# Opening of a two-layer trunk: raw indexer products for four K-tiles, x loaded between modulation tiles, another plan of early chunks

## The chip, the cores and the metric

The kernel runs on one core of a Trainium2 chip. A core has TensorE (PE: matmuls; PEld is its weight load), VectorE (DVE), ScalarE (ACT), GpSimd (POOL), SyncE (SP, which here issues most transfers) and 16 DMA engines. Matmuls accumulate in PSUM, which here is used as eight banks of 128 x 512 fp32: four under the tag "pj", four under the tag "px". The metric is the device time of one execution in microseconds. Each engine works off its instructions in the order in which the program issues them; between engines, semaphores order the work.

## The reference

Two layers (DEPTH 2) of a decoder trunk, 512 tokens, width 2048, fp32:

```python
c_act = silu(c)
for l in range(DEPTH):
    mod = c_act @ w_mod[l] + b_mod[l]               # 2048 x 6144
    shift, scale, gate = split(mod, 3)
    h = rmsnorm(x, norm_gain[l]) * (1 + scale) + shift
    proj = h @ w_in[l]                              # 2048 x 7504
    q_a, k_a, v_a, g_a, q_i, k_i, w_i, q_b, k_b, v_b, g_b = split(proj)
    # group A: indexer (q_i, k_i, w_i) picks 128 keys a query, softmax attention, gate g_a
    # group B: retention of q_b, k_b (rotary), v_b, group norm, gate g_b
    x = x + gate * (concat(y_a, y_b) @ w_out[l])
```

with `rmsnorm(x, g) = x * rsqrt(mean(x*x) + eps) * g`. The factor rsqrt(...) is one number per token and is called rstd here. Shift and scale (with gain) are one number per row of the transposed x.

## The kernel before

**Tiling.** Everything is kept transposed: x as 16 K-tiles of 128 model rows x 512 tokens. fp32 products are made of three fp32r matmuls: a weight w and an activation h are each split into a high part (a copy rounded to fp32r) and a low part (the rest), and wh·hh + wh·hl + wl·hh is summed in PSUM. The high half is made by ScalarE (`split_hi`, line 324; for h, `make_h0`, line 625), the low half by VectorE (`split_lo`, line 334; line 631). Weights come in chunks of up to 1024 columns a partition (`load_chunk`), three tiles of each kind in a ring.

**Modulation.** Shift and scale of layer 0 need 32 tiles of 1 MB from w_mod, one for the shift and one for the scale of each K-tile. VectorE multiplies each with silu(c), broadcast over the partitions (`cb`), and sums along the row (`mod_add`, line 417). Tiles in halves are two such steps. `mod0_loads` issues their transfers, at most four tiles ahead of the sums and into tiles that are free: two of their own, and the arena tiles in which later K-tiles of h will stand. When both sums of a K-tile are there, its h can be made: x is multiplied by rstd (`make_xr`, line 619), ScalarE makes the high part and h itself (lines 625, 629), VectorE the low part (631).

**Opening (`start`).** SP first loads all 16 tiles of x and the positions, then modulation tiles and the first chunks in turn. ScalarE squares x; sums of squares go through TensorE (`row_sums`, line 603), filler matmuls keep it active (`warm`, line 568); `rstd_col` makes 1/sqrt and broadcasts it (line 585). Two units of the bias table (`indicators` on ScalarE, line 894; `unit_mm`, 904; `unit_end`, 911) are made in the gaps. Then K-tile 0 is normalised (`make_h`) and the early plan begins.

**The early plan.** As not all K-tiles are there, projections are done in pieces, listed by hand in PLAN. ("S", c) is chunk c of the group with key, value, indexer key and indexer weights: two K-tiles, 24 matmuls of 336 columns, four PSUM banks "pj" held from S0 to S7. ("E", i, a, b) is K-tiles a to b of 256 columns: for i < 4 of the indexer's queries q_i (384 tokens, as the first 128 need no selection), for i from 4 to 7 of the retention's q and k (512 tokens); each K-tile takes six matmuls, on two banks "px". The result of a first piece is copied to SBUF (`keep`, line 1525), later pieces are added (`more`, line 1540), and the rest of K-tiles, from EARLY[i] on, comes after the plan in full groups (`joined`, line 1532).

**The pacing.** The loop over WORK issues for each plan item: the splits of its weights, its matmuls, the next chunk's transfers and splits, then modulation steps (`mod_step`), then the evacuation. Every item has a cost (1.85 per K-tile of S, 1.36 per K-tile of E); for each RMOD = 4.0 of cost one modulation step is issued, each RBIAS = 6.0 one bias unit. An item whose K-tiles are not yet there forces steps ("forced").

## Time and profile before

| | |
|---|---|
| median of 3 runs | 1851.62 us (1850.3 to 1852.84) |
| the profiled execution's own time | 1849.68 us |
| span of its trace | 1847.9 us, mean granted clock 0.994 |
| TensorE busy in the span | 1821.7 us (99%) |
| VectorE, ScalarE busy | 1384.4 us (75%), 888.0 us (48%) |
| bytes moved | 304.55 MB, mean 165 GB/s |
| modulation sums on VectorE (line 417, 2048 columns) | 2.28 to 2.35 us each |

The profile is of one execution. Its rows give a line of the program, engine, operation, output and input names with shape, a count, busy time and the mean of one; then the idle time ahead of it and what released it. A busy TensorE is not one at its peak: matmuls are pipelined, so their durations overlap, and how many there are counts as much as how long they are.

### The profile page before, as it was taken

How to read it: one execution, taken by the hardware profiler on the slowest of the kernel's cores; microseconds unless marked ns; L12 is line 12 of the kernel's file. 1: busy time of each engine (PE TensorE's matmuls, PEld its weight loads, DVE VectorE, ACT ScalarE, POOL GpSimd, SP SyncE). 2: the span in 40 equal slices, each digit the busy share in tenths (PEclk: the TensorE clock that was granted, in tenths of full speed). 3: DMA queues.
4: the chain of work that ended last, by engine and by line, in shares of the span. 5: the costliest groups of instructions: out<-in, count | busy, mean ns of one | idle time of the engine just before them, and what ended most of it. 6: DMA issues, size and time to landing. Idle time of an engine off the chain costs nothing.

```text
span 1847.9 us, 26300 instructions
## 1 busy us (share of the span) xinstructions
PE 1821.7 (99%) x9644; PEld 1562.9 (85%) x9644; DVE 1384.4 (75%) x2438; ACT 888.0 (48%) x1708; POOL 70.8 (4%) x184
## 2 busy tenths in 40 slices
PE   7999999999999999999999999999999999999998
PEld 7878888888888888888899988888888888889998
DVE  7996699787867846777776699377875686369886
ACT  7668943564546532422235542344444554245443
POOL 0001000000000000100000000000000000000111
PEclk7999999999999999999999999999999999999999
DMA  9995533333454547789864323444534354333554
GB/s 371 364 321 178 165 88 92 109 114 95 123 186 123 174 147 236 233 281 308 304 208 129 103 80 100 142 124 147 155 120 124 93 185 135 102 92 109 149 151 130
DMA packets 175762, 304.55 MB, mean 165 GB/s; under 512 B 16960, under 2 KB 92864, under 8 KB 172048
## 3 DMA queue, kind: packets, MB, share of 16 engines
q1 hardware_dynamic: 171328, 295.23, 50.5%
q0 software_dynamic: 4160, 7.41, 1.6%
q8 instruction: 76, 1.25, 0.3%
q14 instruction: 54, 0.44, 0.1%
q10 hardware_dynamic: 144, 0.22, 0.0%
HBM read 289.18 MB, written 13.63 MB: 164 GB/s over the span
## 4 chain that ended last, share of the span: by engine, by line
PE 83%; DVE 2%; ACT 2%; DMA 1%; issue 1%; SPq 0%; DVEq 0%; ACTq 0%
PE pj L390 15%; PE pj L391 15%; PE pj L392 15%; PE pj L398 6%; PE pj L397 6%; PE pj L396 6%; PE p L1356 3%; PE p L1355 3%; PE p L1354 3%; PE ptr L177 1%; PE pdot L1028 1%; DVE wl L334 1%; PE pdot L1030 1%; ACT wh L324 1%; PE plg L1250 1%
## 5 line engine op out<-in xcount | busy, mean ns | idle before, releaser
L324 ACT ACTIVATE wh<-wf 128x1024 fp32r<-128x1024 f32 (+2 forms) x277 | 284.7, 1029 | 586.9 <-PE pj L391 390.1
L334 DVE TENSOR_TENSOR wl<-wf,wh 128x1024 fp32r<-128x1024 f32 (+2 forms) x277 | 326.6, 1180 | 289.1 <-ACT wh L324 282.5
L390 PE MATMUL pj<-h,wh 128*128 128x512 f32 (+1 forms) x1280 | 488.4, 382 | 1.9 <-ACT bt L911 1.7
L391 PE MATMUL pj<-h,wh 128*128 128x512 f32 (+1 forms) x1280 | 485.9, 380 | 2.6 <-DVE h L631 2.6
L392 PE MATMUL pj<-h,wl 128*128 128x512 f32 (+1 forms) x1280 | 485.7, 379 | 0.5 <-DVE wl L334 0.5
L390 PEld LDWEIGHTS pj<-h,wh 128*128 128x128 f32 x1280 | 240.6, 188 | 44.9 <-issue 2.5
L391 PEld LDWEIGHTS pj<-h,wh 128*128 128x128 f32 x1280 | 240.6, 188 | 42.1 <-DVE h L631 3.8
L392 PEld LDWEIGHTS pj<-h,wl 128*128 128x128 f32 x1280 | 240.5, 188 | 41.4 <-DVE wl L334 1.1
L396 PE MATMUL pj<-wh,h 128*128 128x512 f32 (+1 forms) x616 | 234.6, 381 | 4.1 <-ACT h L625 3.4
L397 PE MATMUL pj<-wl,h 128*128 128x512 f32 (+1 forms) x616 | 233.6, 380 | 0.7 <-DVE wl L334 0.7
L398 PE MATMUL pj<-wh,h 128*128 128x512 f32 (+1 forms) x616 | 232.6, 380 | 0.2 <-DVE h L631 0.2
L396 PEld LDWEIGHTS pj<-wh,h 128*128 128x128 f32 x616 | 116.5, 189 | 26.7 <-ACT h L625 3.9
L397 PEld LDWEIGHTS pj<-wl,h 128*128 128x128 f32 x616 | 116.5, 189 | 20.3 <-DVE wl L334 1.1
L398 PEld LDWEIGHTS pj<-wh,h 128*128 128x128 f32 x616 | 116.2, 189 | 20.4 <-DVE h L631 0.4
L417 DVE CUSTOM_DVE_ANT_0 mw<-mw,cb 128x1024 f32<-128x1024 f32 (+1 forms) x64 | 93.0, 1453 | 7.0 <-POOL mp L416 5.6
L417 DVE CUSTOM_DVE_ANT_0 mw<-mw,cb,mp 128x1024 f32<-128x1024 f32 x68 | 88.3, 1298 | 12.4 <-POOL md L416 7.9
L392 PE MATMUL pj<-y,wl 128*128 128x512 f32 x240 | 93.4, 389 | 0.0
L391 PE MATMUL pj<-y,wh 128*128 128x512 f32 x240 | 93.4, 389 | 0.0
L390 PE MATMUL pj<-y,wh 128*128 128x512 f32 x240 | 93.4, 389 | 0.0
L1262 ACT ACTIVATE bias<-bias,mx 128x128 f32<-128x128 f32 (+1 forms) x64 | 35.9, 561 | 65.3 <-DVE mx L1261 64.6
L1036 DVE SCALAR_TENSOR_TENSOR iacc<-relu,wi,iacc 128x384 f32<-128x384 f32 (+2 forms) x96 | 55.5, 613 | 10.1 <-ACT relu L1034 7.2
L894 ACT ACTIVATE ind<-pos,pt 128x512 bf16<-128x512 f32 (+3 forms) x128 | 61.4, 553 | 0.1
(549 smaller groups left out, 3077.3 us busy)
## 6 DMA issues: line engine op xcount, KB each, us to landing
wf<-in_w_in_dram SPq DMA_DIRECT2D x155, 512.0 KB, 3.7
mw<-in_wmod_dram SPq DMA_DIRECT2D x136, 512.0 KB, 5.7
wf<-in_w_in_dram SPq DMA_DIRECT2D x136, 256.0 KB, 3.1
mw<-in_wmod_dram SPq DMA_DIRECT2D x28, 1024.0 KB, 8.6
wf<-in_w_out_dram SPq DMA_DIRECT2D x32, 512.0 KB, 5.3
...
```

The source lines that it names most:

```text
L324: act(h[:, :n], wf[i][:, :n], AF.Copy)
L334: tt(lo[:, :n], wf.pop(i)[:, :n], f(whl[i][:, :n]), op=OP.subtract)
L390: mm(q, wh[:, o:o + P], ah, start=s0, stop=False)
L391: mm(q, wh[:, o:o + P], al, start=False, stop=False)
L392: mm(q, wl[:, o:o + P], ah, start=False, stop=s1)
L396: mm(q, ah[:, n * P:(n + 1) * P], wh[:, o:o + g.N], start=s0, stop=False)
L397: mm(q, ah[:, n * P:(n + 1) * P], wl[:, o:o + g.N], start=False, stop=False)
L398: mm(q, al[:, n * P:(n + 1) * P], wh[:, o:o + g.N], start=False, stop=s1)
L417: nc.vector.tensor_tensor_reduce(w[:, lo:hi], w[:, lo:hi], cb[:, lo:hi], scale=ng(l, k, 1) if q == 1 else 1.0, scalar=init, op0=OP.mult, o ...
L894: act(v, tab["pos"][:, :w], AF.Sign, bias=tab["pt"][:, col:col + 1], scale=-1.0)
L1036: stt(a[:, :w], r[:, :w], L["WI"][:, c0:c0 + 1], a[:, :w], op0=OP.mult, op1=OP.add)
L1354: mm(dst[m], wh[:, c], bh, start=k == 0 and (own or m == 0), stop=False)
```

## The change

In the opening, the 768 columns of the indexer's queries that belong to E0, E1 and E2 are multiplied for K-tiles 0 to 3 with x·scale before rstd is known, in a group "R" of four chunks of 128 x 768 (NRAW = 3, RAW = 4). `raw_h` makes x·scale, split in high and low, 384 tokens wide, with two more columns that hold the shift; `raw_mm` does 18 matmuls of 386 columns per K-tile on six banks (four "pj", two "px"); `raw_end` copies the six sums to SBUF. Since the sum over K of w·(x·scale·rstd + shift) is rstd times the raw sum plus the shift's column, `raw_join` multiplies by rstd and adds that column and the next piece's sum, when K-tiles 4 to 7 of E0 to E2 are joined.

x is loaded in four lots (1, 3, 6, 6 tiles), each between modulation tiles (`loads`); the squares follow in pairs, in four lots. rstd is known after the last lot; K-tiles 0 to 3 are normalised after that, in a row, by `make_h`. A third bias unit is made in the opening. The first plan item runs when four K-tiles are there. RMOD is 4.5. E0 and E1 go to K-tile 8 early, where they went to 6. Tiles of three early chunks are no longer taken from the general pool (FREE), and the values of h for K-tiles 0 and 1 no longer from VectorE (HVA).

```diff
 DEBUG = False
-PLAN = [("S", 0, 0), ("E", 0, 0, 2, 0), ("S", 0, 1), ("E", 0, 0, 2, 1), ("E", 1, 0, 2),
-        ("E", 2, 0, 2), ("E", 3, 0, 2), ("E", 4, 0, 3), ("E", 5, 0, 3), ("S", 1), ("E", 6, 0, 4), ("E", 7, 0, 4),
-        ("E", 0, 2, 6), ("E", 1, 2, 6), ("S", 2), ("E", 2, 2, 8), ("E", 3, 2, 8), ("S", 3),
-        ("S", 4), ("E", 6, 4, 12), ("E", 7, 4, 12), ("S", 5), ("E", 4, 3, 12), ("E", 5, 3, 12), ("S", 6), ("S", 7)]
+RAW = 4
+NRAW = 3
+
+
+PLAN = [("S", 0), ("S", 1), ("E", 4, 0, 4), ("E", 5, 0, 4), ("E", 6, 0, 4), ("E", 7, 0, 4), ("E", 3, 0, 4), ("S", 2),
+        ("E", 0, 4, 8), ("E", 1, 4, 8), ("E", 2, 4, 8), ("E", 3, 4, 8), ("S", 3), ("E", 6, 4, 8), ("E", 7, 4, 8),
+        ("S", 4), ("S", 5), ("E", 4, 4, 12), ("E", 5, 4, 12), ("E", 6, 8, 12), ("E", 7, 8, 12), ("S", 6), ("S", 7)]
 NE = 8
 EARLY = [max(it[3] for it in PLAN if it[0] == "E" and it[1] == i) for i in range(NE)]
-FREE = (2, 3, 4)
-RMOD = 4.0
+RMOD = 4.5
 RBIAS, KBIAS = 6.0, 3
 REST = [(0, 2, k) for k in range(16)] + [(1, q, k) for k in range(16) for q in (0, 1)] + [(1, 2, k) for k in range(16)]
-HVA = 2
 M0AHEAD = 4
 MX0 = 2
-WA, WS, WL = 24, 4, 8
+WA, WS = 24, 24
 C_ID, C_C, C_CAUS, C_INV, C_THR, C_BLK, C_ONE, C_END = 0, 128, 144, 272, 273, 274, 278, 406
...
     mpart = {}
-    steps0 = [(b, lo, lo + D // 2) for b in range(4) for lo in (0, D // 2)] + [(b, 0, D) for b in range(4, 2 * KT)]
-    m0 = {"load": 0, "add": 0, "mw": 0}
+    whole0 = [b for b in range(4, 2 * KT) if b != 2 * RAW - 1]
+    steps0 = [(b, lo, hi) for b in range(2 * KT) for lo, hi in (((0, D),) if b in whole0 else ((0, D // 2), (D // 2, D)))]
+    m0 = {"load": 0, "add": 0, "mw": 0, "lim": 0}
     m0_tile, m0_last = {}, {}
     def mod0_loads(lim=None):
+        if lim is None:
+            lim = m0["lim"]
         while m0["load"] < len(steps0):
             n = m0["load"]
             b, lo, hi = steps0[n]
             done = steps0[m0["add"]][0] if m0["add"] < len(steps0) else 2 * KT
-            if lim is not None and n >= lim or b >= done + M0AHEAD:
+            if n >= lim or b >= done + M0AHEAD:
                 break
             if lo == 0:
                 keys = [("mw", m0["mw"] % MWBUFS)] + [("HP", j) for j in range(b // 4 + 1, KT // 2)]
         return X[k]
     def make_h0(k, xr):
-        hv = G("hv") if k < HVA else xr
         hh, hl = HLT(k, "h")
         act(hh, xr, AF.Identity, bias=mod_col(0, 0, k), scale=mod_col(0, 1, k))
-        if k < HVA:
-            ts(hv, xr, mod_col(0, 1, k), mod_col(0, 0, k), op0=OP.mult, op1=OP.add)
-        else:
-            act(hv, xr, AF.Identity, bias=mod_col(0, 0, k), scale=mod_col(0, 1, k))
+        act(xr, xr, AF.Identity, bias=mod_col(0, 0, k), scale=mod_col(0, 1, k))
         yield
-        tt(hl, hv, f(hh), op=OP.subtract)
+        tt(hl, xr, f(hh), op=OP.subtract)
         Hh[k], Hl[k] = hh, hl
         yield
+    raw = {}
+
+    def raw_h(k):
+
+        hh, hl = G("rh0", F32R)[:, :TI + 2], G("rl0", F32R)[:, :TI + 2]
+        x, a, b = X[k][:, TOPK:], mod_col(0, 1, k), mod_col(0, 0, k)
+        act(hh[:, :TI], x, AF.Copy, scale=a)
+        act(hh[:, TI:], b.to_broadcast([P, 2]), AF.Copy)
+        stt(hl[:, :TI], x, a, f(hh[:, :TI]), op0=OP.mult, op1=OP.subtract)
+        tt(hl[:, TI:], b.to_broadcast([P, 2]), f(hh[:, TI:]), op=OP.subtract)
+        return hh, hl
+
+    def raw_mm(k, hh, hl):
+        if not k:
+            raw["ps"] = [psum.tile([P, T], F32, name="praw", tag="pj" if n < 4 else "px") for n in range(2 * NRAW)]
+        wh, wl = whl.pop(k)
+        for n, ps in enumerate(raw["ps"]):
+            q, c = ps[:, :TI + 2], slice(n * P, (n + 1) * P)
+            mm(q, wh[:, c], hh, start=k == 0, stop=False)
+            mm(q, wh[:, c], hl, start=False, stop=False)
+            mm(q, wl[:, c], hh, start=False, stop=k == RAW - 1)
+
+    def raw_end():
+        for n, ps in enumerate(raw.pop("ps")):
+            t = raw[n // 2, n % 2] = G("part")
+            act(t[:, :TI + 2], ps[:, :TI + 2], AF.Copy)
+
+    def raw_join(part, key, ps):
+
+        if key in raw:
+            r = raw.pop(key)
+            t = part[key] = r[:, :TI]
+            tt(t, t, state["rstd"][:, TOPK:], op=OP.mult)
+            stt(t, ps, r[:, TI:TI + 1], t, op0=OP.add, op1=OP.add)
+        else:
+            tt(part[key], ps, part[key], op=OP.add)
+
     def start():
         rot, bias = rot_tables(), bias_tables()
-        for k in range(KT):
-            load_x(k)
-        dma(posi, bass.AP(tensor=positions.tensor, offset=positions.offset, ap=[[0, P], [1, T]]))
-        mod0_loads(4)
-        ahead(2, 0)
-        mod0_loads(8)
-        ahead(5, 0)
+        done = 0
+
+        def loads(k):
+            for n in ((0, 1), (4, 5), (8,), (10,))[k]:
+                mod0_loads(n + 1)
+            ahead(k + 1, 0)
+            for j in (range(1), range(1, 4), range(4, 10), range(10, KT))[k]:
+                load_x(j)
+            if k == 0:
+                dma(posi, bass.AP(tensor=positions.tensor, offset=positions.offset, ap=[[0, P], [1, T]]))
+            for n in ((2, 3), (6, 7), (9,), (11, 12))[k]:
+                mod0_loads(n + 1)
+
+        loads(0)
+        loads(1)
         warm(WA)
         act(cs, cst[:, C_C:C_C + KT], AF.Silu)
         act(sm("dummy", 1), cs[:, :1], AF.Sqrt, bias=eps, scale=0.0)
         bias_parts()
         pc = [bcast_c(i) for i in range(4)]
-
-        def put_c(i):
+        for i in range(4):
             v = cb[:, i * T:(i + 1) * T]
             if i % 2:
                 nc.vector.tensor_copy(v, pc[i])
             else:
                 act(v, pc[i], AF.Copy)
-        put_c(1)
-        put_c(3)
+        act(onesr, ones, AF.Copy)
         ind, pend = {}, []
-        def get_ind(u):
-            ind[u] = indicators(*UNITS[u])
-
-        def begin(u):
-            pend.append(unit_mm(*UNITS[u], ind[u]))
-
-        def flush(n=0):
-            while len(pend) > n:
+        def flush():
+            while pend:
                 unit_end(*pend.pop(0))
-
-        pss = psum.tile([P, T], F32, name="prs", tag="pj")
-        ssq, col = G("ssq"), 0
-        for k in range(KT):
-            q = G("sq") if k else ssq
-            act(q, X[k], AF.Square)
-            if k in (3, 5):
-                put_c(k - 3)
-            if k % 3 == 0 and 0 < k < KT - 1:
-                col = row_sums(pss, q, col)
-                warm(WS if k < 12 else WL)
-            elif k:
-                tt(ssq, ssq, q, op=OP.add)
-        col = row_sums(pss, ssq, col)
-        act(onesr, ones, AF.Copy)
-        mod0_add()
-        rstd_col(pss, col, None, "pj")
-        mod0_add()
-        pos_tables()
-        get_ind(0)
-        ahead(3, 0, 1)
-        mod0_add()
-        mod0_add()
-        begin(0)
-        make_h(0, 0, X[0], state["prb"], lambda: ahead(3, 1))
-        copy_rstd()
-        ahead(3, 2)
-        get_ind(1)
-        flush()
-        st.update(have=0, t=RMOD, tb=0.0, done=0)
+        pss, col = PX("prs"), 0
+        for k in range(RAW):
+            for _ in range(1 + (k < 2)):
+                mod0_add()
+            ahead(0, 0, k + 1)
+            for a in ((), (0, 2), (4, 6, 8), (10, 12, 14))[k]:
+                q = [G("sq") for _ in range(2)]
+                for m in range(2):
+                    act(q[m], X[a + m], AF.Square)
+                tt(q[0], q[0], q[1], op=OP.add)
+                col = row_sums(pss, q[0], col)
+            ahead(0, k + 1)
+            if k - 1 in ind:
+                pend.append(unit_mm(*UNITS[k - 1], ind.pop(k - 1)))
+            if k < RAW - 1:
+                for _ in range(1 + (k < 2)):
+                    mod0_add()
+                hh, hl = raw_h(k)
+                flush()
+                if k == 0:
+                    pos_tables()
+                ind[k] = indicators(*UNITS[k])
+                raw_mm(k, hh, hl)
+                if k + 2 < RAW:
+                    loads(k + 2)
+                else:
+                    ahead(RAW + 1, 0)
+                    m0["lim"] = len(steps0)
+                    mod0_loads(m0["load"] + 1)
+            else:
+                mod0_add()
+                flush()
+                warm(WS)
+                rstd_col(pss, col, mod0_add)
+                raw_mm(k, *raw_h(k))
+                copy_rstd()
+        ahead(RAW + 2, 0)
+        make_h(0, 0, X[0], state["rstd"], lambda: ahead(0, RAW + 1))
+        make_h(0, 1, X[1], state["rstd"])
+        raw_end()
+        ahead(RAW + 3, 0)
+        make_h(0, 2, X[2], state["rstd"])
+        make_h(0, 3, X[3], state["rstd"], lambda: ahead(0, RAW + 2))
+        flags.add("early")
+        st.update(have=RAW, t=0.0, tb=0.0, done=RAW)
         hgen, xr = {}, {}
         def get_xr(k):
             if end:
                 hgen[k] = make_h0(k, xr.pop(k))
                 next(hgen[k])
-                if k == 1:
-                    next(hgen.pop(k))
-                    st["have"] = k + 1
             return size
-        st["have"] = 1
-        ahead(7, 2)
         late, after = [], None
         for i, only, kend, cost in WORK:
             while st["have"] < kend:
                 if DEBUG:
                     print("forced", i, st["have"], kend)
                 mod_step()
-            if kend == 2 and len(ind) == NEU:
-                flags.add("early")
-                ahead(5, 4)
-                for u in range(1, NEU):
-                    begin(u)
-                    flush(1)
-                flush()
-                ind.clear()
             end = only is None or only == stream[i][0].kper - 1
             ahead(max(st["done"] + 3, i + 1), max(st["done"] + 1, i + 1))
             chunk_mm(i, only, late)
             parts.append(b)
         tab.update(top=top, parts=parts)
-    UNITS = [(3, 0), (3, 1)]
+    UNITS = [(3, 0), (3, 1), (3, 2)]
     NEU = len(UNITS)
     UNITS += [(j, q) for j in range(NB) for q in range(8) if (j, q) not in UNITS]
         if first:
             def more(key, w):
                 def ev(n, ps):
-                    t = part[key, n]
-                    tt(t, ps[:, :w], t, op=OP.add)
+                    raw_join(part, (key, n), ps[:, :w])
                 return ev
+            g = Group(W_in, [(QI, 256 * NRAW)], 1, "t", 2 * NRAW, hact, None, name="R", kr=(0, RAW))
+            gs += [(g, ch) for ch in range(g.nch)]
             made = {}
             for it in PLAN:
                 only = None
```

More of the change, by code (lines that the diff above doesn't have):

```diff
@@ L303, in load_chunk @@
         g, ch = stream[i]
-        t = G("wf") if i in FREE else ring.tile([P, 1024], F32, name="wf", tag="wf")
+        t = ring.tile([P, 1024], F32, name="wf", tag="wf")
         if g.kind == "7":
@@ L322, in split_hi @@
         n = g.kper * g.N
-        h = G("wh", F32R) if i in FREE else ring.tile([P, 1024], F32R, name="wh", tag="wh")
+        h = ring.tile([P, 1024], F32R, name="wh", tag="wh")
         act(h[:, :n], wf[i][:, :n], AF.Copy)
@@ L332, in split_lo @@
         n = g.kper * g.N
-        lo = G("wl", F32R) if i in FREE else ring.tile([P, 1024], F32R, name="wl", tag="wl")
+        lo = ring.tile([P, 1024], F32R, name="wl", tag="wl")
         tt(lo[:, :n], wf.pop(i)[:, :n], f(whl[i][:, :n]), op=OP.subtract)
```

## The prediction

> **What bounds the kernel now.** I read the page first, then the windows of 10 us over the opening, then the time line of single instructions there, and last the groups by shape.
>
> ```profile
> span 1847.9 us, 26300 instructions
> ...
> PE 1821.7 (99%) x9644; PEld 1562.9 (85%) x9644; DVE 1384.4 (75%) x2438; ACT 888.0 (48%) x1708; POOL 70.8 (4%) x184
> ```
>
> TensorE is 99% busy, so the kernel can only lose what TensorE wastes, and that is looked for in the opening. In the windows the columns are start:end and length, busy time and count of PE, PEld, DVE, ACT and POOL, granted clock, DMA share, GB/s.
>
> ```profile
> 0.00:10.00 10.00, 7.83 (x68) 7.65 (x68) 5.18 (x24) 7.81 (x13) 0.20 (x4) 1.00 0.81 274
> 10.00:20.00 10.00, 7.96 (x48) 7.43 (x48) 7.82 (x13) 6.19 (x13) 0.83 (x1) 0.57 1.04 401
> 20.00:30.00 10.00, 7.43 (x38) 6.11 (x38) 9.49 (x17) 9.93 (x19) 0.00 (x0) 0.58 1.06 387
> 30.00:40.00 10.00, 6.46 (x36) 5.33 (x35) 9.63 (x16) 3.43 (x7) 1.24 (x2) 0.83 1.06 390
> ...
> 60.00:150.00 90.00, 85.50 (x562) 70.57 (x562) 88.52 (x108) 60.66 (x119) 7.90 (x15) 1.00 0.95 331
> ...
> 50.00:177.80 127.80, 123.10 (x796) 101.52 (x795) 110.17 (x143) 93.79 (x187) 12.07 (x23) 1.00 0.86 293
> ```
>
> For 40 us the DMA engines are full; they have moved 2.74, 6.75, 10.62 and 14.52 MB by the ends of the four windows. "Busy" there is mostly filler and stretched matmuls, as the time line shows:
>
> ```profile
> 16.06 0.83 POOL L855 CAST pos<-posi 128x512 f32<-128x512 int32 x1 [15.61 <-DMA posi<-in_positions_dram]
> ...
> 18.32 1.23 DVE L417 CUSTOM_DVE_ANT_0 mw<-mw,cb 128x1024 f32<-128x1024 f32 x1 [0.90 <-DMA mw<-in_wmod_dram]
> ...
> 26.04 0.65 PE L396 MATMUL pj<-wh,h 128*128 128x336 f32 x1
> ...
> 34.47 0.42 PE L396 MATMUL pj<-wh,h 128*128 128x336 f32 x1 [3.39 <-ACT h L625]
> ...
> 39.07 0.33 PE L391 MATMUL pj<-h,wh 128*128 128x384 f32 x1
> ...
> 43.41 0.34 PE L392 MATMUL pj<-h,wl 128*128 128x384 f32 x1
> ...
> 45.96 0.39 PE L390 MATMUL pj<-h,wh 128*128 128x512 f32 x1
> ...
> 47.35 0.39 PE L390 MATMUL pj<-h,wh 128*128 128x512 f32 x1
> ...
> 175.26 0.32 PE L397 MATMUL pj<-wl,h 128*128 128x336 f32 x1
> ...
> 177.24 0.32 PE L398 MATMUL pj<-wh,h 128*128 128x336 f32 x1
> ```
>
> All of x goes first, so the first projection matmul starts at 26.04 and the second K-tile's at 34.47. Start to start, a warm matmul of 384 columns takes (43.41 - 39.07) / 25 = 0.174 us, one of 512 columns (47.35 - 45.96) / 6 = 0.232, one of 336 columns (177.24 - 175.26) / 13 = 0.152. The early plan (S0 to S7 and the partial E chunks) ends at 177.4. It holds 192 matmuls of 336 columns (29.2 us), 168 of 384 (29.2) and 288 of 512 (66.8), together 125.2 us. By 50 us some 24, 51 and 14 of them are done, 15.8 us. So from 50 to 177.4 there are 109.4 us of early plan plus 19 bias units, whose row (busy PE of line 904) is
>
> ```profile
> 50.00:177.80 127.80, 8.91 (x228) 4.01 (x228) 1.00 0.86 293
> ```
>
> thus 12 matmuls and 0.47 us a unit, 8.9 in all: 127.4 - 118.3 = 9.1 us lost after 50, though the window shows only 4.7 idle. VectorE is the cause: from 60 to 150 us it is busy for 88.52 of 90 (the window above), mostly with modulation sums, and K-tile results and low weight halves queue behind them:
>
> ```profile
> 61.47 1.23 DVE L334 TENSOR_TENSOR wl<-wf,wh 128x1024 fp32r<-128x1024 f32 x1
> 62.61 2.28 DVE L417 CUSTOM_DVE_ANT_0 mw<-mw,cb 128x2048 f32<-128x2048 f32 x1
> ...
> 76.65 1.01 DVE L1540 TENSOR_TENSOR part<-pj,part 128x384 f32<-128x384 f32 x2
> 77.58 0.85 DVE L334 TENSOR_TENSOR wl<-wf,wh 128x672 fp32r<-128x672 f32 x1
> 78.34 2.28 DVE L417 CUSTOM_DVE_ANT_0 mw<-mw,cb 128x2048 f32<-128x2048 f32 x1
> ...
> 81.16 0.68 DVE L619 TENSOR_TENSOR xT<-xT,rstd 128x512 f32<-128x512 f32 x1
> ...
> 84.23 1.01 DVE L1540 TENSOR_TENSOR part<-pj,part 128x384 f32<-128x384 f32 x2
> ```
>
> From start to start: low half of a 1024 chunk 1.14, of an S chunk 0.76, two joins 0.93, a first-half modulation step with the previous K-tile's low half 2.82, a second-half step with its x times rstd 3.07.
>
> **The change, part by part.** First the transfers. The bytes up to the second modulation tile of K-tile 2 are now constants 0.29 MB, six modulation tiles 6.29, three chunks of 128 x 768 weights 1.18, ten x tiles 2.62, positions 0.26: 10.64 MB, moved by 30.1 us on the curve above. Landing lags moving: positions (4.74 MB, moved at 15.0) was used at 16.06, the first modulation half (5.27 MB, moved at 16.3) at 18.32, so 1.0 to 2.0; with 1.5 it lands at 31.5. K-tile 3's last half (14.71 MB) lands at 42.0. No semaphore wait stands in SP's queue before that: the tiles are unused arena or ring slots.
>
> K-tiles 0 to 2 thus give bursts of 18 raw matmuls near 15, 24 and 35 us. They lie in time in which TensorE waits for transfers, warm or cold: 18 x 0.174 = 3.1 us, or at the low clock (0.57 and 0.58 in the windows from 10 to 30 us) 3.1 / 0.57 = 5.4, both shorter than the gaps of 9 to 11 us between them.
>
> What decides is when K-tiles 0 to 3 are normalised too, because S0 and S1 head the new plan and need them. The durations:
>
> ```profile
> L631 DVE TENSOR_TENSOR h<-xT,h 128x512 fp32r<-128x512 f32 x14 | 9.6, 686 | 1.1 <-ACT xT L629 1.1
> ...
> L625 ACT ACTIVATE h<-xT,md 128x512 fp32r<-128x512 f32 x15 | 12.2, 815 | 29.1 <-DVE md L421 29.1
> ...
> L324 ACT ACTIVATE wh<-wf 128x768 fp32r<-128x768 f32 x12 | 10.1, 841 | 1.8 <-DMA wf<-in_w_in_dram 1.8
> L675 ACT ACTIVATE sq<-xT 128x512 f32<-128x512 f32 x15 | 9.2, 628 | 0.5
> ...
> L894 ACT ACTIVATE ind<-pos,pt 128x512 bf16<-128x512 f32 x8 | 5.1, 712 | 0.0
> ...
> L1525 ACT ACTIVATE part<-pj 128x384 f32<-128x384 f32 x8 | 3.6, 491 | 3.1 <-PE pj L392 3.1
> ...
> L911 ACT ACTIVATE bt<-pb,top 128x512 f32<-128x512 f32 x2 | 1.3, 670 | 0.0
> ...
> L591 ACT ACTIVATE rstd<-prb 128x256 f32<-128x256 f32 x2 | 0.6, 362 | 0.0
> ...
> L585 PE MATMUL prb<-cst,rcol 128*128 128x128 f32 x8 | 2.1, 441 | 0.9 <-DVE rcol L579 0.9
> ```
>
> Neighbours on ScalarE overlap by some 0.09, so I use 0.09 less than the rows where one follows another. From the landing at 31.5: the sum and its bias add 2.5 (34.0). The split of raw x (386 columns) is not in this trace; its ScalarE part lies between 0.49 (L1525, 384 columns) and 0.82 (L625, 512); I take 0.6, nearer to the equal width, plus 0.25 for the two extra columns: 34.85. Then, in ScalarE's order, one bias evacuation 0.6, four indicators 2.5, the high half of chunk 3 0.75, six squares at 0.54: 41.9. VectorE then adds the last pair 0.6, splits chunk 3 0.87, does the two modulation halves of K-tile 3 at 1.3 each with the reduction 0.1 between, bias add and reciprocal 0.3: 46.4. Transfers alone would give 42.0 + 1.3 + 0.3 = 43.6, so ScalarE's order sets it.
>
> The rstd broadcast (8 matmuls, 2.1 cold, about 1.0 warm) and the two copies (0.36 each, the first beside the second half's matmuls) end at 47.8. Now the four normalisations go back and forth between VectorE and ScalarE in program order: u0 0.65 (like L631's 0.69 for 512 columns, overlapped), high h0 0.8, chunk 4's high half 0.7, its low half 0.8, low h0 0.6, u1 0.65, high h1 0.8 (52.8); six evacuations of the raw sums at 0.43 (55.4); high h2 0.75, low h2 0.65, u3 0.6, high h3 0.8, chunk 5's halves 0.7 and 0.8, low h3 0.6: 60.3. S0 cannot start before, at 53: its four sums need the "pj" banks that the raw sums hold. Raw burst 3 (from 47) and S0 (3.65 us) are hidden in this stretch. So from 60.3 TensorE works without a break of that kind, having done 72 raw (12.5), 24 S0 (3.65) and five of S1 (0.76): 16.9 us. The old kernel is further at that time (15.8 by 50 us). POOL's three early bias stores now leave after S0; nothing here reads them.
>
> Next, the new early plan holds 24 more matmuls of 384 columns (E0 and E1 go to K-tile 8 instead of 6): 24 x 0.174 = 4.2, total 129.4, and that much less later. The joins of the six raw sums have two operations for one: three chunks with two pairs, 0.93 more each. From 60.3 to the low half of S3, VectorE's queue holds gqk 0.3, nine low halves at 1.14 and two at 0.76 (11.8), thirteen modulation steps (one at 2.2, six at 2.82, six at 3.07: 37.5), joins for E0 to E2 (5.6): 55.2, so 115.5. TensorE gets there in S1's rest 2.9, four E chunks at 24 x 0.232 + 0.47 = 6.0, E3 4.6, S2 3.65, four E chunks at 4.2 with three bias units: 60.3 + 53.4 = 113.7; wait 1.8. The next low half waits for a step 3.07 and the joins 0.93 and itself 1.14, against S3's 3.65: wait 1.5. Behind that, TensorE needs 6.0 for each 512-column chunk and VectorE 4.0 to 5.2; no more waits: 3.3. The cover is RMOD 4.5, which spreads 24 sums over 108 us of plan instead of 96; with 4.0 each E chunk (5.44 of plan) would carry 1.36 steps instead of 1.21, 0.45 us more of VectorE. The removed per-tile work (normalised x for four tiles, four FREE loads) was VectorE's and SP's and is in these counts.
>
> End of S7: 60.3 + (129.4 - 16.9) + 20 x 0.47 + 3.3 = 185.5, against 177.4: 8.1 later; less 4.2 of work and one bias unit 0.5 taken from later: **+3.4 us**. Against the profiled execution of 1849.68 that is 1853.1; the median of the runs shown lies 1.94 above that execution, so I forecast **1855.0**. Bounds: lag 1.0 or 2.0 is -0.5 or +0.5; the split of 386 columns -0.1 to +0.2; broadcast cold +1.1; two-operation joins between nothing and 0.93 more per chunk, +/-2.8; waits 0 to 9.1, -3.3 to +5.8.
>
> **The rivals.** *Transfers alone set K-tile 3.* If the six squares get done while ScalarE waits, or transfers run at 401 GB/s from 2 us on with a lag of 1.0 (14.71 MB at 39.7), the reciprocal is at 41.3 instead of 46.4, and if the lighter pacing leaves no wait: 3.4 - 5.1 - 3.3 = -5.0, 1846.6. For it: DMA share 1.04 to 1.06 in those windows. Against: ScalarE's order above.
>
> *VectorE stays the bound (the other side).* Place: E0 to E3, K-tiles 4 to 8. One such chunk needs 1.14 + 1.2 steps at 2.95 + joins 1.9 = 6.6 of VectorE against 4.65 of TensorE. If VectorE enters that stretch with no lead, four chunks lose 2.0 each, and the old 9.1 us stays: 3.4 + 5.8 = +9.2, 1860.8. It decides once low h3 comes some 3 us after 60.3: by then the head start that VectorE gets in E4 to E7 is used up. For it: 110.17 busy of 127.80. Against: the larger RMOD.
>
> *The clock falls between raw burst 3, S0 and S1.* The row of 34.47 shows a matmul after 3.39 us of idle, and by 39.07 the spacing is warm again, so such a gap costs at most half of 4.6, 2.3 us. My gaps are 2 to 3 us; if one reaches 3.4, E4 starts cold: 3.4 + 2.3 = +5.7, 1857.3. Against: the filler of 24 matmuls and raw burst 3 ahead of them. The Trainium skill (TensorE: Matmul & The Clock Gate, "HAM oscillation — how this bites in real kernels") warns of just such bursts with waits between them, and gives some 3.4 us of waiting as what brings the half clock back; the trace agrees as far as the clock of 0.57 between the thin bursts of the old opening goes.
>
> *It doesn't do what it says.* Products are moved ahead, yet the next stage starts no earlier: that is my own forecast, with 16.9 us done at 60.3 against 15.8 at 50 before.
>
> **How the numbers follow.** My forecast 0.47, transfers alone 0.29, VectorE 0.16, clock 0.08. One measurement of this kernel tells about 0.2%, 3.7 us, from no change. The forecast's own range, 1851 to 1859, gives within 0.27, slower 0.19, faster 0.01; transfers: faster 0.26, within 0.03; VectorE: slower 0.15, within 0.01; clock: slower 0.05, within 0.03. Together faster 0.27, within 0.34, slower 0.39. The range reaches the middle of both outer cases: 1845 to 1862.
>
> **What would show it.** Right: raw bursts near 15, 24 and 35 us; reciprocal at 46; low h3 and steady TensorE near 60; S7's end near 185; waits on low halves at S3. Wrong: a reciprocal near 42, S0 running into S1 without a gap, S7's end below 180 (faster), or waits on VectorE of 9 us between 90 and 130 (slower).

## The result and the profile after

The changed kernel takes 1866.15 us (median of four runs, 1865.23 to 1866.38) against 1851.09 (1850.3 to 1852.84) for the kernel before: ratio 1.0079, 95% interval 1.0062 to 1.0097. That is 14.6 us slower by the ratio; the forecast was 1855.0 with a range to 1862. The profiled execution is the one of 1865.23 us. In the experiments below one execution, of the kernel without raw products, took 5983.98 us and is left out of its median. The head of the page:

```profile
span 1863.5 us, 26353 instructions
...
PE 1831.3 (98%) x9672; PEld 1571.3 (84%) x9672; DVE 1391.0 (75%) x2447; ACT 887.4 (48%) x1708; POOL 70.3 (4%) x185
...
PEclk7899999999999999999999999999999999999999
```

The last row in the kernel before:

```profile
PEclk7999999999999999999999999999999999999999
```

The span is 15.6 us longer, TensorE is busy for only 9.6 us more of it, and the granted clock (the row PEclk, 40 slices of 47 us) is now reduced in the second slice as well as in the first. In the windows of 10 us (columns as in the prediction) it is seen where:

```profile
10.00:20.00 10.00, 4.16 (x12) 3.82 (x13) 8.10 (x14) 4.86 (x10) 0.30 (x1) 0.57 1.03 408
20.00:30.00 10.00, 7.08 (x40) 5.23 (x39) 6.70 (x11) 5.58 (x11) 0.69 (x1) 0.67 1.03 406
30.00:40.00 10.00, 7.46 (x52) 6.37 (x50) 6.59 (x10) 5.90 (x13) 0.00 (x0) 0.84 1.03 403
40.00:50.00 10.00, 9.84 (x54) 8.57 (x55) 7.31 (x12) 6.95 (x14) 0.56 (x1) 0.67 1.03 414
50.00:60.00 10.00, 8.01 (x50) 7.68 (x49) 4.89 (x10) 3.68 (x8) 0.54 (x1) 0.71 0.63 207
60.00:70.00 10.00, 8.27 (x41) 7.83 (x42) 6.28 (x11) 8.42 (x18) 0.00 (x0) 0.83 0.33 84
```

To 50 us transfers are full, as before. From 50 to 70 us their share falls to 0.63 and 0.33, the clock stays reduced, and neither VectorE nor ScalarE is full: everything waits for the normalisation of four K-tiles, one step after another. VectorE's time line gives the dates. L422 completes shift and scale of a K-tile, L583 is the reciprocal, L508 the first u (x·scale·rstd of K-tile 0, called u0), L513 the last low half, that of h for K-tile 3 (called low h3):

```profile
14.88 0.16 DVE L422 TENSOR_TENSOR md<-md,mb 128x2 f32<-128x2 f32 x1
...
27.43 0.16 DVE L422 TENSOR_TENSOR md<-md,mb 128x2 f32<-128x2 f32 x1
...
39.12 0.16 DVE L422 TENSOR_TENSOR md<-md,mb 128x2 f32<-128x2 f32 x1
...
51.12 0.16 DVE L422 TENSOR_TENSOR md<-md,mb 128x2 f32<-128x2 f32 x1
51.20 0.17 DVE L583 RECIPROCAL rcol<-rcol 128x4 f32<-128x4 f32 x1
...
55.68 0.75 DVE L508 SCALAR_TENSOR_TENSOR u<-xT,md,rstd 128x512 f32<-128x512 f32 x1 [2.97 <-ACT rstd L595]
...
67.39 0.75 DVE L513 SCALAR_TENSOR_TENSOR h<-u,md,h 128x512 fp32r<-128x512 f32 x1
```

The K-tiles come every 12 us, the reciprocal 4.8 us later than forecast, the last low half at 68.1 instead of 60.3. The kernel before has its K-tile 3 at 56.5, 11.6 us sooner than the changed one (its line 631 makes the low halves from K-tile 1 on, at 34.45, 47.93 and here):

```profile
55.80 0.69 DVE L631 TENSOR_TENSOR h<-xT,h 128x512 fp32r<-128x512 f32 x1
```

TensorE's time line shows what it waits for: raw products for the split of x, S0 for the evictions of the raw banks, and late in the plan once more for a bank.

```profile
15.84 0.69 PE L653 MATMUL praw<-rh,wh 128*128 128x386 f32 x1 [7.87 <-ACT rh L642]
...
28.39 0.69 PE L653 MATMUL praw<-rh,wh 128*128 128x386 f32 x1 [1.96 <-ACT rh L642]
...
40.07 0.69 PE L653 MATMUL praw<-rh,wh 128*128 128x386 f32 x1 [2.26 <-ACT rh L642]
...
50.69 2.72 PE L572 MATMUL pw<-wz 128*128 128x128 bf16 x24 [0.78 <-ACT bt L950]
53.20 2.02 PE L589 MATMUL prb<-cst,rcol 128*128 128x128 f32 x8
...
61.25 0.42 PE L397 MATMUL pj<-wh,h 128*128 128x336 f32 x1 [2.55 <-ACT part L660]
...
123.71 0.44 PE L391 MATMUL pj<-h,wh 128*128 128x384 f32 x1 [3.10 <-ACT bt L950]
...
196.89 0.32 PE L399 MATMUL pj<-wh,h 128*128 128x336 f32 x1
```

S7's last matmul ends at 197.05 (its start and one spacing of 0.152; 177.4 before), 19.65 later. The span grows by 15.6, so 4.05 of that comes back, as E0 and E1 have been taken further. How much of this arises before 70 us is reckoned from the counts of matmuls in the window from 0 to 70 us, times the spacings of the prediction. The three rows of the kernel before are those of its lines 390 (every third matmul of E; 391 and 392, the other two, have 42 each), 396 (every third of S) and 904 (bias units, 12 each); the three of the changed kernel are lines 653 (every third raw one), 397 (S; 398 has 14 too, 399 has 13) and 943 (units):

```profile
0.00:70.00 70.00, 16.01 (x43) 8.22 (x43) 0.85 1.02 375
...
0.00:70.00 70.00, 6.43 (x16) 3.83 (x16) 0.85 1.02 375
...
0.00:70.00 70.00, 3.01 (x48) 1.09 (x48) 0.85 1.02 375
```

```profile
0.00:70.00 70.00, 11.68 (x24) 6.87 (x24) 0.76 0.84 312
...
0.00:70.00 70.00, 5.15 (x14) 3.22 (x14) 0.76 0.84 312
...
0.00:70.00 70.00, 3.54 (x36) 0.76 (x36) 0.76 0.84 312
```

Before: 127 matmuls of E (48 of 384 columns, 79 of 512: 26.7 us), 48 of S (7.3), four units (1.9), together 35.9 us of work, 34.1 lost. After: 72 raw (12.5), 41 of S (6.2), three units (1.4), 20.2 us of work, 49.8 lost. So 15.7 us more are lost by 70 us. From there to the end of S7 the changed kernel loses 7.4 us: 127.05 less 110.7 of the plan (129.4 - 12.5 - 6.2) and 8.9 for 19 units at 0.47. The old one loses 8.2 there, 107.4 less 91.2 and 17 units at 0.47, 8.0. The loss is in the opening.

### The profile page after: what moved, and what is told of

Same layout as the page of the kernel before. It is cut to its first block, busy times and chain, and to the rows that moved or that the text cites. A ratio compares the mean times of both kernels' runs of the same rounds, so it can differ in the third digit from the quotient of the medians.

```text
span 1863.5 us, 26353 instructions
## 1 busy us (share of the span) xinstructions
PE 1831.3 (98%) x9672; PEld 1571.3 (84%) x9672; DVE 1391.0 (75%) x2447; ACT 887.4 (48%) x1708; POOL 70.3 (4%) x185
## 4 chain that ended last, share of the span: by engine, by line
PE 87%; DVE 5%; ACT 4%; issue 1%; DMA 1%; SPq 0%; DVEq 0%; ACTq 0%
PE pj L391 16%; PE pj L393 16%; PE pj L392 16%; PE pj L397 7%; PE pj L398 7%; PE pj L399 7%; PE p L1395 3%; PE p L1394 3%; PE p L1393 3%; DVE wl L335 1%; DVE mw L418 1%; PE ptr L178 1%; PE pdot L1067 1%; ACT wh L325 1%; PE pdot L1069 1%
## 5 line engine op out<-in xcount | busy, mean ns | idle before, releaser
L391 PE MATMUL pj<-h,wh 128*128 128x512 f32 (+1 forms) x1256 | 480.5, 383 | 3.3 <-ACT bt L950 3.1
L393 PE MATMUL pj<-h,wl 128*128 128x512 f32 (+1 forms) x1256 | 478.3, 381 | 0.5 <-DVE wl L335 0.5
L392 PE MATMUL pj<-h,wh 128*128 128x512 f32 (+1 forms) x1256 | 478.3, 381 | 0.0
L391 PEld LDWEIGHTS pj<-h,wh 128*128 128x128 f32 x1256 | 236.4, 188 | 45.7 <-ACT bt L950 3.4
L393 PEld LDWEIGHTS pj<-h,wl 128*128 128x128 f32 x1256 | 236.4, 188 | 41.5 <-DVE wl L335 1.3
L392 PEld LDWEIGHTS pj<-h,wh 128*128 128x128 f32 x1256 | 236.3, 188 | 39.0 <-issue 0.4
L399 PEld LDWEIGHTS pj<-wh,h 128*128 128x128 f32 x616 | 115.9, 189 | 20.2
L1301 ACT ACTIVATE bias<-bias,mx 128x128 f32<-128x128 f32 (+1 forms) x64 | 35.9, 561 | 66.2 <-DVE mx L1300 65.5
L933 ACT ACTIVATE ind<-pos,pt 128x128 bf16<-128x128 f32 (+3 forms) x128 | 61.3, 556 | 0.1
```

What stands on the lines that cost most here:

```text
L391: mm(q, wh[:, o:o + P], ah, start=s0, stop=False)
L392: mm(q, wh[:, o:o + P], al, start=False, stop=False)
L393: mm(q, wl[:, o:o + P], ah, start=False, stop=s1)
L399: mm(q, al[:, n * P:(n + 1) * P], wh[:, o:o + g.N], start=False, stop=s1)
L933: act(v, tab["pos"][:, :w], AF.Sign, bias=tab["pt"][:, col:col + 1], scale=-1.0)
```

## Experiments

All times are medians; the ratio is to the kernel before on the same chip. Each interval reaches 0.0015 to 0.002 (3 to 4 us) to both sides, so differences below some 3 us between two of these kernels are told apart by their traces, not by their times. "Behind" is the ratio's excess times 1851 us; the changed kernel is 14.6 behind.

| run | time, us | ratio [interval] | behind, us |
|---|---|---|---|
| changed kernel | 1866.15 | 1.0079 [1.0062, 1.0097] | 14.6 |
| no units in the opening | 1860.51 | 1.0050 [1.0035, 1.0065] | 9.3 |
| half the bytes of the first modulation tiles | 1865.99 | 1.0080 [1.0065, 1.0095] | 14.8 |
| no raw products | 1868.3 | 1.0093 [1.0073, 1.0113] | 17.2 |
| no filler | 1865.11 | 1.0076 [1.0061, 1.0091] | 14.1 |
| normalisation reordered | 1861.52 | 1.0054 [1.0039, 1.0069] | 10.0 |
| squares summed by TensorE | 1868.73 | 1.0094 [1.0079, 1.0109] | 17.4 |
| three edits together | 1863.79 | 1.0067 [1.0052, 1.0082] | 12.4 |
| no units in the plan | 1864.70 | 1.0072 [1.0055, 1.0089] | 13.3 |
| no units in the opening, reordered | 1857.50 | 1.0042 [1.0027, 1.0057] | 7.8 |
| kernel before with the new plan | 1862.42 | 1.0068 [1.0053, 1.0083] | 12.6 |
| rstd multiplied on GpSimd | 1864.59 | 1.0077 [1.0061, 1.0094] | 14.3 |
| no units, reordered, GpSimd | 1855.93 | 1.0033 [1.0020, 1.0046] | 6.1 |

Theory A is that the alternation of ScalarE and VectorE within each K-tile sets the pace of 12 us; rival B that transfers do; rival C that the raw products are worth what they hold and are not the trouble; rival D that the filler ahead of the broadcast is needed, as it keeps the clock up.

The theory comes from this stretch, ScalarE's and VectorE's time lines between the shift and scale of K-tile 1 and of K-tile 2:

```profile
28.24 0.67 ACT L950 ACTIVATE bt<-pb,top 128x512 f32<-128x512 f32 x1
28.81 2.55 ACT L933 ACTIVATE ind<-pos,pt 128x512 bf16<-128x512 f32 x4
31.26 0.84 ACT L325 ACTIVATE wh<-wf 128x768 fp32r<-128x768 f32 x1
32.00 3.22 ACT L715 ACTIVATE sq<-xT 128x512 f32<-128x512 f32 x6
39.31 0.61 ACT L641 ACTIVATE rh<-xT,md 128x384 fp32r<-128x384 f32 x1 [4.10 <-DVE md L422]
```

```profile
28.88 2.28 DVE L418 CUSTOM_DVE_ANT_0 mw<-mw,cb 128x2048 f32<-128x2048 f32 x1
...
33.17 0.69 DVE L716 TENSOR_TENSOR sq<-sq 128x512 f32<-128x512 f32 x1 [2.00 <-ACT sq L715]
...
35.86 0.95 DVE L335 TENSOR_TENSOR wl<-wf,wh 128x768 fp32r<-128x768 f32 x1
36.73 2.35 DVE L418 CUSTOM_DVE_ANT_0 mw<-mw,cb,cst 128x2048 f32<-128x2048 f32 x1
```

VectorE ends its first modulation sum at 31.2, then waits 2.00 for squares that stand on ScalarE behind a bias evacuation and four indicators; the second modulation sum, at 36.73, waits for no transfer, it stands in the queue behind pair sums and the low half. Then ScalarE waits 4.10 for VectorE.

### No bias units in the opening

```diff
-    UNITS = [(3, 0), (3, 1), (3, 2)]
+    UNITS = []
...
-                ind[k] = indicators(*UNITS[k])
```

> The changed kernel without its three early bias units: no indicators, matmuls or evacuations of them in the opening; all 32 units are made later, in the early plan and behind it. Theory A (a chain on ScalarE and VectorE: per K-tile the split of raw x, a bias evacuation 0.67, four indicators 2.55, a high half, squares, then on VectorE pair sums, a low half and the next modulation sums): the reciprocal comes about 6 us earlier, at 45 instead of 51.2, where the transfers take over; the last low half of h for K-tile 3 at 62 instead of 67.4; the three units cost 1.5 us of TensorE later: 1860 to 1863 us. Rival B (x lies behind modulation tiles, the transfers are late): reciprocal within 1 us of 51.2, time 1865 to 1868 us.

1860.51, ratio 1.0050: theory A's outcome. The dates move as it says:

```profile
45.42 0.17 DVE L583 RECIPROCAL rcol<-rcol 128x4 f32<-128x4 f32 x1
...
59.02 0.74 DVE L513 SCALAR_TENSOR_TENSOR h<-u,md,h 128x512 fp32r<-128x512 f32 x1
```

The reciprocal is 5.8 us earlier, low h3 8.4 (at 59.8, sooner than the 62 that I expected). Only 5.3 arrive in the time; the three units' 1.4 us of TensorE are still to be done later.

### Half the bytes of the first modulation tiles

```diff
-whole0 = [b for b in range(4, 2 * KT) if b != 2 * RAW - 1]
+whole0 = range(2 * RAW, 2 * KT)
...
+            if b >= 2 * RAW or lo == 0:
                 dma(m0_tile[b][:, lo:hi], wmod[b][:, lo:hi])
```

(The second sum of each of these tiles reads the first half again.)

> The changed kernel with half of the bytes of the first eight modulation tiles left out: only the first half of each is loaded, and the second half's sum reads the first half's products again (so shift and scale of K-tiles 0 to 3 are not the reference's); all eight tiles are summed as two halves. 4.2 MB, some 10 us of transfers, less ahead of K-tile 3. Theory A (engine chain): reciprocal at 50.5 to 52, time 1865 to 1868 us. Rival B (late transfers): reciprocal 5 to 10 us earlier, time 1856 to 1861 us.

1865.99: nothing. From 10 to 50 us the DMA share falls from 1.03 to 0.87, yet the reciprocal stays at 51.31:

```profile
10.00:50.00 40.00, 28.47 (x154) 23.91 (x154) 29.10 (x51) 23.26 (x43) 1.29 (x3) 0.68 0.87 338
```

Rival B falls.

### No raw products

E0 to E2 of K-tiles 0 to 3 become items of the plan behind E3; `raw_h`, `raw_mm` and the group R are left out.

```diff
-("E", 3, 0, 4), ("S", 2),
+("E", 3, 0, 4), ("E", 0, 0, 4), ("E", 1, 0, 4), ("E", 2, 0, 4), ("S", 2),
...
-                hh, hl = raw_h(k)
...
-                raw_mm(k, hh, hl)
```

> The changed kernel without the raw products: x still behind the modulation, K-tiles 0 to 3 normalised together, and E0 to E2 of K-tiles 0 to 3 are ordinary plan items behind E3. 12.5 us of matmuls move from the waits of the opening into the steady part. Theory A: the chain loses the splits of raw x, of the raw weights and six evacuations, so low h3 comes at about 58.6 instead of 67.4, and the pacing over more plan eases VectorE by some 3 us: 1864 to 1869 us, so the raw products are worth next to nothing as placed. Rival C (the raw products pay their 12.5 us and something else costs the loss): 1875 to 1879 us.

1868.3 (median of three runs), 17.2 behind: the 12.5 us of TensorE's work that the raw products take forward bring 2.6 us, less than the interval. Rival C falls. A part of the rest goes into their splits and evacuations: without them the reciprocal is at 48.34 and low h3 at 64.2 instead of 68.1, 3.9 us sooner. Where the other 6 us go was not followed.

### No filler ahead of the broadcast

```diff
-WA, WS = 24, 24
+WA, WS = 24, 0
```

> The changed kernel without the 24 filler matmuls ahead of the rstd broadcast. Theory A: the broadcast starts at the reciprocal, 51.4 instead of 53.2, and everything behind it 1.8 us earlier: 1863.5 to 1865 us. Rival D (the filler keeps the clock up for raw burst 3 and S0): same or slower, 1866 to 1869 us.

1865.11, 0.1 above theory A's range. u0 starts at 54.06 instead of 55.68, low h3 comes 1.6 earlier; the time falls by 0.5 to 1.0, less than the interval. It does not rise, so rival D falls, and the filler is at most a small part of the loss.

### The normalisation reordered

```diff
-        make_h(0, 0, X[0], state["rstd"], lambda: ahead(0, RAW + 1))
-        make_h(0, 1, X[1], state["rstd"])
-        raw_end()
-        ahead(RAW + 3, 0)
-        make_h(0, 2, X[2], state["rstd"])
-        make_h(0, 3, X[3], state["rstd"], lambda: ahead(0, RAW + 2))
+        for k in range(RAW):
+            stt(us[k], X[k], mod_col(0, 1, k), state["rstd"], op0=OP.mult, op1=OP.mult)
+        hi(0); hi(1); lo(0); lo(1)
+        raw_end(0, 4)
+        ahead(0, RAW + 1)
+        hi(2); hi(3); lo(2); lo(3)
+        raw_end(4, 6)
+        ahead(RAW + 3, RAW + 2)
```

(`hi` is the high half on ScalarE, `lo` the low half on VectorE; WS = 0 as in the run before.)

> The same work as the changed kernel, but between the reciprocal and the planned early work: no filler matmuls, the four products u0 to u3 first on VectorE, high halves h0 and h1, then the evictions of the first four raw banks, then the splits of the next weight chunk, h2, h3 and the last two evictions. Theory N (of the 15 us some 4 to 6 arise behind the reciprocal, because u, high h and low h of the four K-tiles alternate between VectorE and ScalarE with the weight splits and the six evictions between them): the reciprocal stays at about 51, the first matmul of S0 comes at 58 to 60 instead of 61.3, the last low half of h3 at 61 to 63 instead of 67.4, and the time falls by 3 to 5.5 us, to 1860.5-1863. Rival M (S0's banks, freed by the evictions behind the last raw burst, set the start whatever the order of the h): low h3 comes earlier, the time stays within 1.3 us of the run without filler, 1864-1866.

1861.52, 10.0 behind: theory N's outcome. The reciprocal is no earlier (52.09), but the stretch behind it shrinks; VectorE's low halves h2 and h3, and TensorE's first matmul of S0:

```profile
60.08 1.41 DVE L753 SCALAR_TENSOR_TENSOR h<-u,md,h 128x512 fp32r<-128x512 f32 x2
```

```profile
59.32 0.42 PE L397 MATMUL pj<-wh,h 128*128 128x336 f32 x1 [0.18 <-ACT wh L325]
```

From the first u to the last low half it takes 6.7 us (54.84 to 61.5), where it took 12.5 (one weight split of 0.86 now comes behind), because none waits for its neighbour on the other engine. Rival M is out: the time falls, and S0's banks come 2 us earlier too.

### Squares summed by TensorE

```diff
-                tt(q[0], q[0], q[1], op=OP.add)
-                col = row_sums(pss, q[0], col)
+                    col = row_sums(pss, q, col)
```

> The changed kernel with the eight additions of pairs of squares (0.69 us each on VectorE) left out; TensorE sums each square by itself, 32 more one-column matmuls, in time in which it is idle. Theory A (the alternation of ScalarE and VectorE in each K-tile sets the pace of K-tiles 1 to 3): the scale and shift of K-tile 3 and the reciprocal come 3 to 5.5 us earlier (46 to 48 instead of 51.2), the time falls by 2.5 to 5.5, to 1860.5-1863.5. If ScalarE alone sets the pace (its splits, indicators and squares add up whatever VectorE does), the reciprocal moves by less than 1.5 us and the time stays at 1864.5-1866.

1868.73: neither outcome. K-tile 2's shift and scale are indeed 4.5 us earlier (34.61), but the reciprocal is 3.3 later (54.51). The first two lines are VectorE's, the third is TensorE's group of the row sums between 14 and 58 us:

```profile
34.61 0.16 DVE L422 TENSOR_TENSOR md<-md,mb 128x2 f32<-128x2 f32 x1
...
52.13 0.22 DVE L579 TENSOR_REDUCE rcol<-prs 128x4 f32<-128x64 f32 x1 [4.34 <-PE prs L607]
```

```profile
L607 PE MATMUL prs<-cst,sq 128*128 128x1 f32 x128 | 18.0, 276 | 0.7 <-ACT sq L715 0.7
```

The 32 more one-column matmuls (64 more records) bring TensorE's time on row sums from 7.9 to 18.0 us, between raw bursts at a low clock, and make it the engine that the reciprocal waits for. So theory A holds for VectorE's share, and TensorE has no 10 us to spare there: my expectation that it was idle was wrong.

### The three edits together

The edits of the sections on units, on the reordered normalisation and on TensorE's sums.

> The changed kernel with three edits together: no bias units in the opening, squares summed by TensorE alone, and the reordered normalisation without filler. If the causes add (theories A and N): reciprocal at 42.5 to 44.5, low h3 at 52 to 55, time 1850 to 1855, so level with the kernel before or up to 4 us behind it. If transfers set K-tile 3 as soon as the alternation is shorter (they are at their full share from 10 to 50 us without the units): reciprocal not under 44.5, time 1855 to 1858.

1863.79, neither outcome and worse than two of its parts: the reciprocal is at 50.53 here, where it is at 45.4 without units, since the row sums on TensorE take it back.

### No units in the plan

```diff
-RBIAS, KBIAS = 6.0, 3
+RBIAS, KBIAS = 1e9, 3
```

> The changed kernel with no bias units among the planned early work (behind 70 us); the units run later, where the layer's other fillers run. If the wait of 3.1 us for the bank of a bias unit at 123.7 us and the half-clock stretch behind it are a cause of the loss: time falls by 3 to 5 us, to 1861-1863. If the early stretch behind 70 us is no part of the loss (useful work there took the same in the kernel before, by my count): within 1.5 us of the changed kernel, 1864.5-1867.5.

1864.70, the second outcome, and within the interval of no change against the changed kernel. The wait at 123.7 us isn't tied to the units: without them TensorE waits 1.64 at 116.67 and 3.17 at 125.69, both for low weight halves on VectorE. The unit's bank was only where the late VectorE showed.

### No units in the opening, and the normalisation reordered

> The changed kernel with two edits together: no bias units in the opening, and the reordered normalisation without filler (the squares stay summed in pairs on VectorE). If theories A and N are two separate parts of the loss, their gains (5.6 and 4.6 us against 1866.15) add: 1855 to 1857.5, with the reciprocal at about 45 and the last low half of h3 at 54 to 56. If a third limit takes over (the transfers, at their full share from 10 to 50 us once the units are out, or the evictions of the raw banks): 1858 to 1860.5.

1857.50, 7.8 behind: 6.8 of the 14.6 are taken back by making the units later, reordering the normalisation and leaving out the filler, against 9.9 if the gains had added: at the edge of the first outcome, and within the intervals. Low h3 is there at 55.1, S0 runs from 52.96. That is 1.4 us sooner than the kernel before has its K-tile 3 (56.5), and yet this kernel is 7.8 us behind it. So how soon K-tile 3 comes does not explain the loss by itself.

### The kernel before, with the new order of chunks

```diff
-PLAN = [("S", 0, 0), ("E", 0, 0, 2, 0), ("S", 0, 1), ("E", 0, 0, 2, 1), ("E", 1, 0, 2),
-        ("E", 2, 0, 2), ("E", 3, 0, 2), ("E", 4, 0, 3), ("E", 5, 0, 3), ("S", 1), ("E", 6, 0, 4), ("E", 7, 0, 4),
...
+PLAN = [("S", 0, 0), ("S", 0, 1), ("S", 1), ("E", 0, 0, 4), ("E", 1, 0, 4), ("E", 2, 0, 4), ("E", 4, 0, 4), ("E", 5, 0, 4),
+        ("E", 6, 0, 4), ("E", 7, 0, 4), ("E", 3, 0, 4), ("S", 2),
...
-FREE = (2, 3, 4)
+FREE = ()
```

(From ("S", 2) on the plan is that of the changed kernel. RMOD stays 4.0.)

> The kernel before with its own opening (squares first, K-tile 0 normalised at about 34 us, no raw products), but with the changed kernel's order of early chunks, in which S0 and S1 are followed by products over four K-tiles; the first early chunks use the ring's three buffers, and the first three E items follow S1. Theory P (the loss before 70 us is that the plan can only begin in earnest with K-tile 3, whose low half comes at 65.5 us in the kernel before and at 68.1 in the changed one, so that what TensorE did from 34 to 66 us on one, two and three K-tiles is gone, and the raw products put back less than half of it): the time is 1861 to 1868, near the changed kernel without raw products (1868.7). Rival O (the loss comes from the changed opening itself, the new order of chunks costs nothing): 1850 to 1854.

1862.42, 12.6 behind: the time of theory P; rival O falls. With the old opening, no raw product, no late rstd, the new order (with the three buffers that came with it) costs most of what the change costs. The 65.5 us in the expectation is the low half of K-tile 4 in the kernel before; its K-tile 3 is there at 56.5 (and the 34 us is its K-tile 1). In this run K-tile 3 comes sooner still, at 51.2:

```profile
50.55 0.69 DVE L631 TENSOR_TENSOR h<-xT,h 128x512 fp32r<-128x512 f32 x1
```

So it is not a later K-tile 3 that costs the time here. TensorE's time line shows what does (both are of an execution of 1865.43, 3.0 above the median):

```profile
34.70 0.43 PE L396 MATMUL pj<-wh,h 128*128 128x336 f32 x1 [4.19 <-ACT h L625]
...
41.55 0.47 PE L396 MATMUL pj<-wh,h 128*128 128x336 f32 x1 [3.00 <-ACT h L625]
...
45.41 0.65 PE L398 MATMUL pj<-wh,h 128*128 128x336 f32 x1 [3.11 <-DVE h L631]
...
49.32 0.65 PE L396 MATMUL pj<-wh,h 128*128 128x336 f32 x1 [3.27 <-ACT h L625]
```

K-tile by K-tile S0 and S1 wait for the next h; in the kernel before, pieces of E0 to E5 over the K-tiles already there fill just these gaps, and from 35 to 56 us it waits no longer than 0.93 at once. By 70 us this kernel has done 72 matmuls of E (12.5), 48 of S (7.3) and five units (2.4), 22.2 us, and lost 47.8, against 34.1 before and 49.8 in the changed kernel.

### The multiplication by rstd on GpSimd

```diff
-            tt(t, t, state["rstd"][:, TOPK:], op=OP.mult)
...
             act(t[:, :TI + 2], ps[:, :TI + 2], AF.Copy)
+            nc.gpsimd.tensor_tensor(t[:, :TI], t[:, :TI], state["rstd"][:, TOPK:], op=OP.mult)
```

> The changed kernel with the multiplication of the six raw sums by rstd moved from VectorE (six of 0.55 us between 104 and 126 us) to GpSimd, behind the evictions of the raw banks at about 60 us. If VectorE's added work in E0 to E2 is part of the loss: the wait of 3.1 us at 123.7 us falls under 1.5 us and the half-clock stretch behind it goes, the time falls by 2 to 4, to 1862-1864. If the wait only goes to another place: within 1.3 us, 1865-1867.5.

1864.59, between the two outcomes and within the interval of no change, but the trace shows both a gain and a loss. (It is of an execution of 1862.41, 2.2 below the median.) TensorE's wait at the bank falls from 3.10 to 0.91 and the clock between 110 and 130 us is 1.00 instead of 0.91: in this execution at least, the multiplications in VectorE's joins were the cause of most of that wait. The loss is in the opening; GpSimd's line, VectorE's and TensorE's:

```profile
61.36 7.35 POOL L661 TENSOR_TENSOR part<-part,rstd 128x384 f32<-128x384 f32 x6 [50.03 <-ACT part L660]
```

```profile
61.59 1.50 DVE L508 SCALAR_TENSOR_TENSOR u<-xT,md,rstd 128x512 f32<-128x512 f32 x1
```

```profile
123.02 0.44 PE L391 MATMUL pj<-h,wh 128*128 128x384 f32 x1 [0.91 <-ACT bt L950]
```

While GpSimd works, VectorE's u takes 1.50 instead of 0.75, and low h3 is 2 us later (70.1).

### No units, reordered, and GpSimd

> The two edits of the opening and the multiplication on GpSimd together. If all three are separate parts of the loss: 1852 to 1854.5. If the wait behind 110 us only goes elsewhere: as with the two edits of the opening alone, 1855 to 1857.5.

1855.93, 6.1 behind, in the range of the second outcome: the best of the changed forms, not told apart from the one without GpSimd, and still slower than the kernel before (interval 1.0020 to 1.0046). None of these kernels beats it.

## Why the prediction was wrong

The direction came out, the size did not: +15.6 us of span instead of +3.4. The sum was built on dates, and they can be compared one by one.

**The failed step** is the start of the chain: "From the landing at 31.5: the sum and its bias add 2.5 (34.0)", with raw bursts "near 15, 24 and 35 us". I worked out ScalarE's and VectorE's order for K-tile 3 only and let transfers set K-tiles 1 and 2. But that order holds in every K-tile. The bursts came at 15.84, 28.39 and 40.07, K-tile 2's shift and scale at 39.3 instead of 34.0. The sum for K-tile 3, 12.4 from there to the end of the reciprocal, was right (39.3 to 51.4, 12.1), and so would 12 us for each of the two before have been. This is 4.8 us at the reciprocal. Taking the units out gives as much back (5.8 us at the reciprocal, 3.9 of them already at K-tile 2's shift and scale, 5.3 in the time); taking bytes out gives nothing.

**Mis-sized terms.** Broadcast and copies, 1.4 in the sum, took 4.5 from the reciprocal to u0: filler, itself held 0.78 by a unit, stood in TensorE's queue until 53.2, and the broadcast was cold, 2.02. That is 3.1, where I had allowed 1.1 upward; without the filler 1.6 of it is gone. The going back and forth of the normalisation, 12.5 in the sum, took 12.5, step by step within 0.3 of the sum. Behind low h3 the plan took 128.9 to S7's end, where I had 125.2: 3.7 more. It is 7.5 lost where I had 3.3 (and one bias unit fewer): 3.6 of waits, 3.1 of them at 123.71 and not at S3, 1.75 of half clock behind that wait, and some 2 that I have not placed. Later work came back as 4.05, not 4.7. Together 4.8 + 3.1 + 3.7 + 0.6 = 12.2, the whole difference between 15.6 and 3.4.

**What the sum did not ask.** "Products are moved ahead, yet the next stage starts no earlier" was my forecast in words, and that was so. But I took the new order of chunks as given. The kernel before with this order is 12.6 us behind, although its K-tile 3 then comes 5.3 us sooner. With its own order TensorE did 35.9 us of work by 70 us, 20.4 of it in pieces of S0 and of E0 to E5 that need at most three K-tiles; the new one leaves that time open until four K-tiles are normalised, and the raw products, meant to fill it, return 2.6 us by the time, or bring the work by 70 us to 20.2 against 35.9. The two findings are not in conflict: given the plan, each step ahead of K-tile 3 stands on the path, which is why the chain's length counted.

**Rivals.** *Transfers alone* falls: with a DMA share of 0.87 the reciprocal is where it was. *VectorE stays the bound* shows at its place, but with 3.6 us of waits and not 9: low h3 came 7.8 us after my 60.3, past the 3 us from which I had it decide, and most of the wait at 123.7 goes with the joins' multiplications. It is seen in the order of the queues, ScalarE's and then VectorE's:

```profile
121.64 0.81 ACT L628 ACTIVATE h<-xT,md 128x512 fp32r<-128x512 f32 x1 [5.89 <-DVE md L422]
...
123.20 0.45 ACT L950 ACTIVATE bt<-pb,top 128x256 f32<-128x256 f32 x1
```

```profile
119.05 2.35 DVE L418 CUSTOM_DVE_ANT_0 mw<-mw,cb,cst 128x2048 f32<-128x2048 f32 x1
```

The evacuation of a bank stands behind an h that waits 5.89 for a modulation sum. It replaces waits of like size in the kernel before (4.6 us in all from 70 us to the end of S7, 3.6 in the changed kernel), so it adds little: 7.4 lost behind 70 us against 8.2. *The clock falls* came true, with shorter gaps than the 3.4 that I had asked for. Behind the 2.55 ahead of S0 the granted clock is 0.51 from 62.5 to 66 us; that costs little, as S0's stretch is covered by the normalisation. Behind the 3.10 at 123.71 12 matmuls ran 0.32 apart instead of 0.174, 1.75 us. The Trainium skill (TensorE: Matmul & The Clock Gate, "HAM oscillation — how this bites in real kernels") gives some 3.4 us of waiting; here 2.55 and 3.10 were enough.

**Left open.** The old order of chunks with the raw products was not tried; the four low halves come within 8.7 us of each other there (59.4 to 68.1), so pieces over fewer K-tiles would have little room. How much of the 12.6 us of the new order belongs to the ring's three buffers for the first chunks, which came with the new order, was not separated.
